# RMSNorm and matmul on one core: token tiles grouped by six where they were grouped by eight

## The chip, the core and the metric

The kernel runs on one core of one Trainium2 chip. The time is the device time of one execution in microseconds (us). The kernel before was run eight times; its median is 211.32 us, the lowest 211.1 and the highest 211.99.

## The reference

```
batch, seq, dim, out_dim = 16, 1024, 512, 768
rms = np.sqrt(np.mean(x ** 2, axis=-1, keepdims=True) + eps)
x_norm = x / rms * gamma
return np.matmul(x_norm, weight).astype(np.float32)
```

There are 16,384 tokens of 512 float32 values. Each token is divided by its root mean square, multiplied by gamma, and multiplied by a 512 x 768 weight matrix. The input is 33.5 MB, the weight 1.6 MB and the output 50.3 MB.

## The kernel before

A token tile is 128 tokens, one on each partition; there are NT = 128 of them. Tiles are worked off in pairs j = 0 to 63 (tile i belongs to pair i // 2).

For one pair the stages are these. GpSimd casts the two tiles from float32 to bf16 into a buffer `xb` (`cast`, line 86, four buffers of one pair). TensorE transposes the pair with two float32-wide transposes per tile, each word holding two bf16 values (`transpose_word`, line 113). VectorE copies the transposed pair from PSUM to `xT` (`evac`, line 120). ScalarE squares each tile of `x` with a running sum (`square`, line 90) and takes the root; VectorE takes the reciprocal (lines 94 and 96). TensorE multiplies each tile with the bf16 weights, which carry gamma, in four steps of 128 rows, 512 and 256 columns wide (`matmul`, line 147). ScalarE finishes the even tiles and VectorE the odd ones: the product times the reciprocal root goes to the output tile `ot` in SBUF (`scale`, lines 130 and 132).

Loads and stores move a group of tiles at once. In `rows` (line 54) a group of n tiles is laid out so that each partition holds n consecutive tokens: a load is 128 rows of n x 2 KB and a store 128 rows of n x 3 KB, each row contiguous in HBM. The group size G is 8, so a full load has rows of 16 KB and a full store rows of 24 KB. The first two and the last two groups of eight are cut into smaller transfers by the table `parts` (line 45). The pool `xin` has five buffers of eight tiles for loads, `out` three buffers of eight tiles for stores (lines 58 and 65).

All loads and all stores, and the two loads of the weights, are issued by the SP engine, one after the other in program order, on one DMA queue. SP waits before a store until the last tile of its group is finished (`store`, line 142), and everything that comes later in program order waits behind it. Loads are placed by `load_until(2 * j + AHEAD)` at the top of the loop over pairs (line 259), with AHEAD = 20: the load that begins at tile s comes in program order at the top of pair (s - 18) / 2. Before the loop, tiles 0 to 23 are requested (lines 185 to 189).

The order of the instructions is the written one (`tc.manual_schedule()`, line 177). In the loop, pair j casts pair j + 3, takes the norms of pair j + 1, and feeds the transposes of pair j + 2 in between its own matmuls (lines 258 to 277). The last pair's two tiles are finished in two column parts each (lines 280 to 286).

Of the kernel before, what the change touches and what calls it, by code (L numbers as in the profile page):

```python
# [12 lines left out]
F32 = mybir.dt.float32  # L13
# [5 lines left out]
def kernel(  # L19
# [9 lines left out]
    P = 128  # L29

    x = x.flatten_outer_dims()
    out = out.flatten_outer_dims()
    N, D = x.shape
    _, O = out.shape
    K = D // P
    NT = N // P
    NP = NT // 2
    G = 8
    NG = NT // G
    AHEAD = 20  # L40
    WIDE = 512

    parts = {0: [1, 2, 1, 2, 2], 1: [4, 4], NG - 2: [4, 4], NG - 1: [2, 2, 2, 1, 1]}
    first, size = {}, {}
    for g in range(NG):
        i = g * G
        for n in parts.get(g, [G]):
            for t in range(n):  # L50
                first[i + t], size[i + t] = i, n
            i += n

    def rows(ap, i):
        return ap[first[i] * P:(first[i] + size[i]) * P, :].rearrange("(p t) d -> p t d", t=size[i])

    singles = ctx.enter_context(tc.tile_pool(name="singles", bufs=1))
    xin = ctx.enter_context(tc.tile_pool(name="xin", bufs=5))
    xbp = ctx.enter_context(tc.tile_pool(name="xb", bufs=4))
    junk = ctx.enter_context(tc.tile_pool(name="junk", bufs=2))  # L60
    stats = ctx.enter_context(tc.tile_pool(name="stats", bufs=4))
    xt_pool = ctx.enter_context(tc.tile_pool(name="xt", bufs=4))
    tpsum = ctx.enter_context(tc.tile_pool(name="tpsum", bufs=2, space=bass.MemoryType.PSUM))
    opsum = ctx.enter_context(tc.tile_pool(name="opsum", bufs=3, space=bass.MemoryType.PSUM))
    outp = ctx.enter_context(tc.tile_pool(name="out", bufs=3))

    x_tiles, xb_tiles, tp_tiles, rstd_of, xT_tiles, o_tiles = {}, {}, {}, {}, {}, {}

    def held(tiles, i, n=1):
        return tiles[i // G][:, i % G:i % G + n, :]  # L70

    def load(i):
        if i // G not in x_tiles:
            x_tiles[i // G] = xin.tile([P, G, D], F32, name="xt")
        nc.sync.dma_start(out=held(x_tiles, i, size[i]), in_=rows(x, i))  # L75

    starts = [i for i in range(NT) if first[i] == i]
# [1 line left out]
    def load_until(i):  # L79
        while starts and starts[0] < i:  # L80
            load(starts.pop(0))

    def cast(i, engine, n=1):
        if i // 2 not in xb_tiles:
            xb_tiles[i // 2] = xbp.tile([P, 2, D], BF16, name="xb")
        engine.tensor_copy(out=xb_tiles[i // 2][:, i % 2:i % 2 + n, :], in_=held(x_tiles, i, n))  # L86

    def square(i, ssq):
        jk = junk.tile([P, D], BF16, name="jk")
        nc.scalar.activation(out=jk, in_=held(x_tiles, i)[:, 0, :], func=AF.Square, accum_out=ssq)  # L90
# [44 lines left out]
        return opsum.tile([P, 2, WIDE], F32, name="ops").rearrange("p a b -> p (a b)")  # L135

    def out_tile(i):
        if i // G not in o_tiles:
            o_tiles[i // G] = outp.tile([P, G, O], F32, name="ot")
        return o_tiles[i // G][:, i % G, :]  # L140

    def store(i):
        if i == first[i] + size[i] - 1:
# [14 lines left out]
    def finish_tile(i, acc, engine):  # L158
        scale(engine, out_tile(i), acc[:, :O], rstd_of[i])
        store(i)  # L160
# [16 lines left out]
    with tc.manual_schedule():  # L177
# [102 lines left out]
        for i in (NT - 2, NT - 1):  # L280
            for lo, hi, engine in ((0, WIDE, nc.scalar), (WIDE, O, nc.vector)):
                a = accumulator()
                for k in range(K):
                    matmul(i, k, a, lo, hi)
                scale(engine, out_tile(i)[:, lo:hi], a[:, lo:hi], rstd_of[i])
            store(i)
# [35 lines left out]
```

## Time and profile before

| what | value |
|---|---|
| median of eight runs | 211.32 us |
| the profiled execution's own time | 211.18 us |
| its span, first to last instruction | 209.4 us |
| lies around the span | 1.8 us |
| mean granted TensorE clock | 0.991 |
| bytes moved by the DMA engines | 85.69 MB |

The profile follows one execution. The span is what the instruction records cover; the time is 1.8 us longer. PE is TensorE's matmul and transpose work, DVE is VectorE, ACT ScalarE, POOL GpSimd, and SP the engine that only issues transfers here; SPq is its sequencer. A group of instructions is one row: line, engine, operation, what it writes and reads, count, busy time and mean length, and then the idle time before it with what ended it. The rows of DMA issues give the count, the size of each and the median time from issue to landing. "DMA share" in a table by stretches is the mean busy share of the core's 16 DMA engines; it can come out a little over 1 because packets on one engine overlap slightly.

### The profile page before, as it was taken

The numbers are of one execution on the slowest core, as the hardware profiler recorded it, in microseconds if no ns is written. First come the engines' busy times: TensorE is split into PE (matmuls) and PEld (weight loads), VectorE is DVE, ScalarE is ACT, GpSimd is POOL, SyncE is SP. The second block draws the span as 40 slices with busy tenths as digits, with TensorE's granted clock in tenths as the row PEclk, the third lists the DMA queues.
The fourth block names the chain that finished last, engine by engine and source line by source line (L and its number), as shares of the span: only waits on it lengthen the run. The fifth ranks groups of instructions, "written<-read, shape, count | busy, mean of one in ns | idle before, by whom it ended". The sixth has DMA issues, their size and how long they took to land.

```text
span 209.4 us, 3573 instructions
## 1 busy us (share of the span) xinstructions
PE 199.5 (95%) x1272; PEld 137.5 (66%) x1297; DVE 111.6 (53%) x204; ACT 158.2 (76%) x388; POOL 66.5 (32%) x71
## 2 busy tenths in 40 slices
PE   7999999999999999999999999999999999999970
PEld 2466767666776667766777666766677666776640
DVE  2555654564465456545644654565466456545630
ACT  4589787788778777877887787778778777877840
POOL 1157432516232433323242332324233315050000
PEclk9999999999999999999999999999999999999996
DMA  6999999999999999999999999999999999998984
GB/s 215 409 426 424 382 441 412 425 423 450 419 412 443 421 433 415 427 444 410 440 416 433 427 435 430 430 424 426 435 423 432 415 436 390 420 447 350 410 355 163
DMA packets 8070, 85.69 MB, mean 409 GB/s; under 512 B 1138, under 2 KB 1140, under 8 KB 3956
## 3 DMA queue, kind: packets, MB, share of 16 engines
q1 hardware_dynamic: 7776, 85.46, 97.3%
q8 instruction: 10, 0.16, 0.3%
q10 hardware_dynamic: 276, 0.00, 0.1%
q14 instruction: 8, 0.07, 0.1%
HBM read 35.13 MB, written 50.33 MB: 408 GB/s over the span
## 4 chain that ended last, share of the span: by engine, by line
PE 92%; DMA 3%; issue 1%; DVE 0%; SPq 0%; DVEq 0%
PE ops L147 79%; PE tp L113 13%; DMA w_f<-in_weight_dram 3%; SPq L75 0%; DVE w_bf L132 0%; DVE ot L132 0%; DVEq L132 0%
## 5 line engine op out<-in xcount | busy, mean ns | idle before, releaser
L147 PE MATMUL ops<-w_bf,xT 128*128 128x512 bf16 (+1 forms) x999 | 192.5, 324 | 1.4 <-DVE w_bf L132 0.2
L147 PEld LDWEIGHTS <-xT 128*128 128x128 bf16 x1024 | 100.2, 98 | 56.5 <-DVE xT L120 0.8
L86 POOL CAST xb<-xt 128x1024 bf16<-128x1024 f32 (+1 forms) x65 | 65.8, 1020 | 120.3 <-DMA xt<-in_x_dram 64.8
L120 DVE COPY xT<-tp 128x1024 bf16<-128x1024 bf16 (+1 forms) x67 | 44.6, 667 | 80.9 <-PE tp L113 80.9
L130 ACT ACTIVATE ot<-ops,rstd 128x768 f32<-128x768 f32 (+1 forms) x65 | 58.1, 895 | 37.6 <-PE ops L147 36.8
L90 ACT ACTIVATE jk<-xt 128x512 bf16<-128x512 f32 x128 | 78.7, 619 | 1.3 <-DMA xt<-in_x_dram 1.3
L113 PE MATMUL tp<-ident_f,xb 128*128 128x128 f32 x256 | 69.0, 273 | 0.6 <-DVE xb L86 0.5
L132 DVE TENSOR_SCALAR ot<-ops,rstd 128x768 f32<-128x768 f32 (+1 forms) x65 | 64.5, 992 | 2.9 <-PE ops L147 2.8
L113 PEld LDWEIGHTS tp<-ident_f,xb 128*128 128x128 f32 x256 | 35.7, 141 | 5.3 <-issue 1.1
L90 ACT ACTIVATION_READ_ACCUMULATOR jk<-xt 128x1 f32 x128 | 24.4, 191 | 0.0
L94 ACT ACTIVATE rms<-ssq,eps_sb 128x2 f32<-128x2 f32 (+1 forms) x64 | 18.9, 296 | 2.0
L96 DVE RECIPROCAL rstd<-rms 128x2 f32<-128x2 f32 (+1 forms) x64 | 10.0, 156 | 3.2 <-ACT rms L94 3.1
L202 PE MATMUL ops<-warm 128*128 128x512 bf16 x15 | 5.0, 479 | 1.2 <-DVE eps_sb L195 1.2
L130 ACT ACTIVATE w_bf<-w_f,g_sb 128x768 bf16<-128x768 f32 x2 | 1.9, 936 | 2.2 <-DMA w_f<-in_weight_dram 2.2
L202 PEld LDWEIGHTS <-warm 128*128 128x128 bf16 x15 | 1.5, 113 | 2.9 <-DVE eps_sb L195 1.2
L184 ACT ACT_TABLE_LOAD x1 | 1.3, 1283 | 1.8 <-issue 1.8
L86 DVE CAST xb<-xt 128x512 bf16<-128x512 f32 x2 | 0.9, 428 | 2.4 <-DMA xt<-in_x_dram 2.4
L132 DVE TENSOR_SCALAR w_bf<-w_f,g_sb 128x512 bf16<-128x512 f32 (+2 forms) x3 | 1.4, 485 | 1.4 <-DMA w_f<-in_weight_dram 1.4
L193 DVE MEMSET warm<- 128x256 uint32 x1 | 0.3, 272 | 0.9 <-PEq L303 0.9
L224 PEld LDWEIGHTS tp<-ident_f,g_row 2*128 2x128 f32 x2 | 0.3, 201 | 0.3 <-DVE xT L120 0.3
L224 PE MATMUL tp<-ident_f,g_row 2*128 2x2 f32 x2 | 0.4, 265 | 0.1
masks.py:199 POOL TENSOR_SCALAR_AFFINE_SELECT ident_f<-ident_f 128x128 f32<-128x128 f32 x1 | 0.3, 293 | 0.1
(7 smaller groups left out, 0.8 us busy)
## 6 DMA issues: line engine op xcount, KB each, us to landing
out_dram<-ot SPq DMA_DIRECT2D x12, 3072.0 KB, 15.9
xt<-in_x_dram SPq DMA_DIRECT2D x12, 2048.0 KB, 20.3
out_dram<-ot SPq DMA_DIRECT2D x4, 1536.0 KB, 11.3
out_dram<-ot SPq DMA_DIRECT2D x6, 768.0 KB, 8.9
xt<-in_x_dram SPq DMA_DIRECT2D x4, 1024.0 KB, 14.1
xt<-in_x_dram SPq DMA_DIRECT2D x6, 512.0 KB, 14.7
w_f<-in_weight_dram SPq DMA_DIRECT2D x2, 768.0 KB, 6.9
out_dram<-ot SPq DMA_DIRECT2D x4, 384.0 KB, 8.8
```

What stands on the lines that cost most here:

```text
L86: engine.tensor_copy(out=xb_tiles[i // 2][:, i % 2:i % 2 + n, :], in_=held(x_tiles, i, n))
L90: nc.scalar.activation(out=jk, in_=held(x_tiles, i)[:, 0, :], func=AF.Square, accum_out=ssq)
L94: nc.scalar.activation(out=rms[:, :n], in_=ssq[:, :n], func=AF.Sqrt, scale=1.0 / D, bias=eps_sb)
L96: nc.vector.reciprocal(out=rstd[:, :n], in_=rms[:, :n])
L113: nc.tensor.transpose(out=tp_tiles[j][:, t, h, :], in_=words[:, lo:lo + P], identity=ident_f)
L120: nc.vector.tensor_copy(out=dst[:, t:t + n, :], in_=src[:, t:t + n, :])
L130: nc.scalar.mul(out=dst, in_=src, mul=r)
L132: nc.vector.tensor_single_scalar(out=dst, in_=src, scalar=r, op=mybir.AluOpType.mult)
L147: nc.tensor.matmul(out=acc[:, lo:hi], lhsT=xT_tiles[i // 2][:, i % 2, k // 2, :, k % 2], rhs=w_bf[:, k, lo:hi], start=(k == 0), stop=(k == ...
L184: nc.scalar.preload_act_table(AF.Sqrt)
L202: nc.tensor.matmul(out=spare[:, :WIDE], lhsT=warm[:, :P], rhs=warm, start=True, stop=True)
L224: nc.tensor.transpose(out=gp[:, c, :], in_=g_row[:, :, c], identity=ident_f[:2, :2])
```

## The change

The group size becomes 6, and the grouping is no longer by i // 8 but by an explicit list. A full load now has rows of 12 KB and a full store rows of 18 KB. `xin` goes from five buffers of eight tiles to six of six (80 KB to 72 KB per partition), `out` from three of eight to four of six (72 KB per partition both times). AHEAD stays 20.

The list of transfers was 1, 2, 1, 2, 2, 4, 4, then twelve of 8 (tiles 16 to 111), then 4, 4, 2, 2, 2, 1, 1. It becomes 1, 2, 1, 2, 2, 4, then eighteen of 6 (tiles 12 to 119), then 2, 2, 2, 1, 1. That is 29 loads and 29 stores instead of 26 and 26. The new dictionary `base` gives the first tile of the buffer that a tile lives in; a buffer holds one inner list of `parts`.

```diff
-    G = 8
-    NG = NT // G
+    G = 6
     AHEAD = 20
     WIDE = 512
...
-    parts = {0: [1, 2, 1, 2, 2], 1: [4, 4], NG - 2: [4, 4], NG - 1: [2, 2, 2, 1, 1]}
-    first, size = {}, {}
-    for g in range(NG):
-        i = g * G
-        for n in parts.get(g, [G]):
+    parts = [[1, 2, 1, 2], [2, 4]]
+    while sum(map(sum, parts)) + G < NT - 2:
+        parts.append([G])
+    parts += [[2, 2, 2], [1, 1]]
+    first, size, base = {}, {}, {}
+    i = 0
+    for group in parts:
+        start = i
+        for n in group:
             for t in range(n):
-                first[i + t], size[i + t] = i, n
+                first[i + t], size[i + t], base[i + t] = i, n, start
             i += n
+    assert i == NT
...
-    xin = ctx.enter_context(tc.tile_pool(name="xin", bufs=5))
+    xin = ctx.enter_context(tc.tile_pool(name="xin", bufs=6))
...
-    outp = ctx.enter_context(tc.tile_pool(name="out", bufs=3))
+    outp = ctx.enter_context(tc.tile_pool(name="out", bufs=4))
...
     def held(tiles, i, n=1):
-        return tiles[i // G][:, i % G:i % G + n, :]
+        t = i - base[i]
+        return tiles[base[i]][:, t:t + n, :]
 
     def load(i):
-        if i // G not in x_tiles:
-            x_tiles[i // G] = xin.tile([P, G, D], F32, name="xt")
+        if base[i] not in x_tiles:
+            x_tiles[base[i]] = xin.tile([P, G, D], F32, name="xt")
         nc.sync.dma_start(out=held(x_tiles, i, size[i]), in_=rows(x, i))
...
     def out_tile(i):
-        if i // G not in o_tiles:
-            o_tiles[i // G] = outp.tile([P, G, O], F32, name="ot")
-        return o_tiles[i // G][:, i % G, :]
+        if base[i] not in o_tiles:
+            o_tiles[base[i]] = outp.tile([P, G, O], F32, name="ot")
+        return o_tiles[base[i]][:, i - base[i], :]
```

## The prediction

> **What bounds the kernel now.** I read the page first: the span, the busy shares, the DMA row, the chain.
>
> ```profile
> span 209.4 us, 3573 instructions
> PE 199.5 (95%) x1272; PEld 137.5 (66%) x1297; DVE 111.6 (53%) x204; ACT 158.2 (76%) x388; POOL 66.5 (32%) x71
> DMA  6999999999999999999999999999999999998984
> DMA packets 8070, 85.69 MB, mean 409 GB/s; under 512 B 1138, under 2 KB 1140, under 8 KB 3956
> q1 hardware_dynamic: 7776, 85.46, 97.3%
> PE 92%; DMA 3%; issue 1%; DVE 0%; SPq 0%; DVEq 0%
> ```
>
> Two resources are full at once. TensorE makes up 92% of the chain, and the 16 DMA engines are 90% busy or more in nearly every slice. The table by stretches says how close they are and what happens at the end:
>
> ```profile
> core 0: us, PE busy (x) PEld busy (x) DVE busy (x) ACT busy (x) POOL busy (x), PEclk, DMA share, GB/s
> 84.30:96.45 12.15, 12.10 (x81) 8.52 (x81) 6.75 (x12) 9.67 (x25) 4.17 (x4) 1.00 1.01 427
> ...
> 192.50:194.00 1.50, 1.50 (x13) 1.04 (x11) 0.32 (x2) 0.91 (x2) 0.00 (x0) 1.00 0.59 238
> ...
> 199.00:200.00 1.00, 1.00 (x8) 0.61 (x7) 0.00 (x0) 0.84 (x1) 0.00 (x0) 1.00 0.73 301
> ...
> 206.10:208.40 2.30, 0.00 (x0) 0.00 (x0) 0.00 (x0) 0.00 (x0) 0.00 (x0) 0.50 0.10 40
> ```
>
> Eight tiles take TensorE 12.15 us (1.519 each); their 3 MB store and 2 MB load take the DMA engines the same 12.15 us. In 192.5 to 200 some engines run dry before a store arrives. But in 206.1 to 208.4 the share is 0.10, or 1.6 engines of 16: one or two engines are still writing when the others are done. The last row says when they finish: the last store, issued by SP at 203.39, lands 5.2 us later, at 208.6, and the span ends there.
>
> ```profile
> 203.39 0.33 SPq L144 DMA_DIRECT2D out_dram<-ot  x1
> out_dram<-ot SPq DMA_DIRECT2D x1, 384.0 KB, 5.2
> ```
>
> The landing records, one per engine and transfer, show the same: 14 of the 16 parts of the last store land by 206.5, two at 208.2 and 208.6. These two fell behind at 23 to 37 us and have no idle time afterwards: the last five stores land on them at 201.0, 203.0, 204.8, 206.7, 207.7, then 208.6, spaced by packet time alone. So the end is set by the sum of the packets on the two late engines, not by TensorE, whose last product is at 202.8.
>
> **What one row costs.** The page counts 7776 packets on the queue. That is 54 transfers (26 loads, 26 stores, 2 of weights) times 128 rows and 16 completion writes: a row is one packet whatever its length, and an engine gets 8 rows of each transfer. The trace's single packets have these median lengths: stores of 3, 6, 12 and 24 KB 121, 234, 460 and 912 ns; loads of 2, 4, 8 and 16 KB 84, 159, 313 and 611 ns; a completion 9 ns. Two 12 KB stores take 920 against 912, so a store row costs 8 ns beside its bytes; for loads two of 8 KB against one of 16 gives 15, two of 4 KB against one of 8 gives 5.
>
> **The change, part by part.**
>
> *Six more transfers.* Three loads x 8 rows x 5 to 15 ns = 0.12 to 0.36 us; three stores x 8 x 8 = 0.19; six completions x 9 = 0.05. Sum on every engine, the late ones included: 0.36 to 0.60; I take 0.5 us, as most of the new load rows are long, where the overhead was 15. Here the Trainium skill speaks against the change: "DMA: Bandwidth & Descriptors", on the anatomy of one DMA (measured for transfers issued by GpSimd), gives about 2.0 us fixed per transfer plus bytes over 436 GB/s. By it a middle group before would take 2 x 2.0 + 5.24 MB / 436 = 16.0 us, where the trace has 12.15, and six more transfers would cost 12 us. The fixed part is not paid on the engines here, since the next transfer is already queued. The rows decide: 0.5.
>
> *Middle groups.* Store 8 x 686 ns (18 KB, on the line through 12 and 24) + load 8 x 461 (12 KB as for stores) + 18 ns = 9.20 us; the same arithmetic gives 12.20 before, where 12.15 was seen, so 9.16. TensorE needs 6 x 1.519 = 9.11. The DMA engines fall behind by about 0.05 us per group, 0.8 over 18 groups; 0.3 of that is won back in the pieces that are gone.
>
> *Loads are requested later.* Before, the load of tile s is released by the store that ends at tile s - 25, so 24 tiles ahead (36.5 us); after, by the one that ends at s - 19, 18 ahead (27.3 us). That is 9.1 us less lead. In return eight fewer tiles of loads are queued in front when the request is made: 8 x 611 ns = 4.9 us. What lead is spare now?
>
> ```profile
> 47.48 0.38 SPq L75 DMA_DIRECT2D xt<-in_x_dram  x1
> xt<-in_x_dram SPq DMA_DIRECT2D x1, 2048.0 KB, 20.1
> 67.70 1.04 POOL L86 CAST xb<-xt 128x1024 bf16<-128x1024 f32 x1 [2.96 <-DMA xt<-in_x_dram]
> ```
>
> Tile 48 is requested at 47.48, lands at 67.6, and is cast until 68.7. Its transposes come with tile 44, which starts at about 76.3 (tile 16 at 33.75, then 1.519 each): 7.5 us spare, 7.2 in later groups. After: 7.2 - 9.1 + 4.9 = 3.0, falling to about 2.2 by the last group. TensorE should not wait. GpSimd waits longer for the load and has 2 us idle per pair to do so.
>
> *Buffers.* A load into `xin` reuses a buffer read at least 12 tiles before (six of six, 18 ahead); an output buffer is written again 18 tiles, 27 us, after its store is issued, which lands in about 12 to 16. Cost nothing; if a store took over 27 us, ScalarE's and VectorE's writes and then TensorE would wait.
>
> *Start.* Still tiles 0 to 23 are requested in eight loads. Tiles 12 and 13 come in a load of six rather than four and land 16 x 77 ns = 1.2 us later, so their cast moves from 18.0 to 19.2; their transposes come with tile 9, at 23. Nothing. The load of tile 24 is two tiles shorter, 1.2 us earlier.
>
> *Tail.* Tiles 114 and 115 now leave with 119. For the 14 engines that are idle at 193, work from there is 5.5 + 3 x 1.89 + 2 x 0.98 = 13.1 us, to 206.7 instead of 206.1. The late two have 3.9 us of work left at 192.8 (the store of 112 to 115 lands at 197.2); they will have 3.9 - 1.9 + 0.5 = 2.5, so they don't run dry and merely end 0.5 later.
>
> Sum: the profiled 211.18 + 0.5 = 211.7; the median stands 0.14 higher, so **211.8 us**, +0.2%. Within 0.2% (0.42 us) is about what measurement can't tell from no change.
>
> **Rivals.**
>
> *Long packets go away (faster).* The 16 KB loads average 625 ns against a median of 611; several groups took over 1 us at 19 to 21 us and again at 29 to 33, just when the two engines fell behind. The 8 KB loads average 313.6 against 313. The skill's same page, among latency facts, reports rates falling where rows are a large power of two apart in HBM, measured from 512 KB; 16 KB is a power of two and 12 is not, but no trace here shows that this matters. If 12 KB loads have no long packets, 14 ns x 96 rows = 1.3 us are saved: 211.32 + 0.5 - 1.3 = 210.5. The bound is the punctual engines: at most 2.1 - 0.6 = 1.5 us off, 209.8. Against it: long packets also hit the 24 KB stores (mean 920), and some sit beside instruction fetches, which stay.
>
> *The rows are slower than the line says, and loads come late (slower).* If a group takes over 9.11 + 3.0 / 18 = 9.28 us (1.4% over my 9.16), the spare lead is used up within the run and TensorE waits for GpSimd's cast. At 2% over, 18 x 0.18 = 3.3 us more packet time on engines that never idle: 211.32 + 0.5 + 3.3 = 215.1; at 1.4%, 214.1. Against it: 12 KB rows were seen, at 460.
>
> *It does nothing measurable.* Where an engine falls behind depends on which one meets a fetch or a long packet; half a microsecond less of that hides the extra rows: 211.3.
>
> **How the numbers follow.** My forecast 0.50 (it straddles the bound: slower 0.27, same 0.23); long packets gone 0.25 (faster 0.19, same 0.06); late loads 0.15, slower; nothing 0.10 (same 0.06, slower 0.04). Faster 0.19, same 0.35, slower 0.46. The forecast's own range is 211.3 to 212.3. For 8 in 10 the range goes from 210.3 (most of the faster case) to 213.6 (just short of the late case).
>
> **What would show it.** Right: TensorE without waits on `xb`; middle loads landing about 15.5 to 16.5 us after their issue; 18 KB packets near 686 ns and 12 KB ones near 461; one or two engines writing alone for some 2 us at the end. Wrong: TensorE waiting for line 86 in the middle (late loads); all 16 engines ending together near 206.7 (long packets gone); DMA share falling in the middle.

## The result, and the profile after

The changed kernel takes 212.51 us (median of 11 runs, 212.31 to 213.21) where the kernel before takes 211.26 us (32 runs). The ratio is 1.0058, with a 95% interval of 1.0044 to 1.0072: about 1.2 us slower. The forecast was 211.8 us, 0.5 us slower. The result lies inside the range given for 8 in 10 (210.3 to 213.6), and 0.2 us above the forecast's own range (211.3 to 212.3).

These lines of the changed kernel's page answer to those shown of the kernel before:

```profile
span 210.6 us, 3587 instructions
PE 199.7 (95%) x1272; PEld 137.9 (65%) x1297; DVE 111.7 (53%) x204; ACT 158.3 (75%) x388; POOL 64.7 (31%) x71
DMA  6999999999999999999999999999999999996993
q1 hardware_dynamic: 8640, 85.46, 97.0%
PE 92%; DMA 1%; DVE 1%; ACT 1%; issue 1%
```

The span grew by 1.2 us, and no engine's own work grew by more than 0.2 us. The queue's 8640 packets are 60 transfers x (128 + 16), as counted. Their time per DMA engine is 97.0% of 210.6 = 204.3 us, against 97.3% of 209.4 = 203.7.

TensorE did not wait for GpSimd's casts: its list of waits has no `xb` in it.

```profile
PE ops L207 <- DVE eps_sb L200: 1.2, 1, 1.2
PE tp L229 <- DVE xT L125: 0.3, 1, 0.3
```

SP issues the last store at the same moment as before, 203.39, and it lands 6.2 us later instead of 5.2. So TensorE is not late; what was lost shows between the last product and the last byte.

```profile
203.39 0.33 SPq L149 DMA_DIRECT2D out_dram<-ot  x1
out_dram<-ot SPq DMA_DIRECT2D x1, 384.0 KB, 6.2
```

The table by stretches of the changed kernel, with the columns as before:

```profile
192.50:194.00 1.50, 1.50 (x13) 1.04 (x11) 0.32 (x2) 0.92 (x3) 0.00 (x0) 1.00 0.64 238
...
206.10:208.40 2.30, 0.00 (x0) 0.00 (x0) 0.00 (x0) 0.00 (x0) 0.00 (x0) 0.73 0.45 178
208.40:210.60 2.20, 0.00 (x0) 0.00 (x0) 0.00 (x0) 0.00 (x0) 0.00 (x0) 0.50 0.02 8
```

The engines again run dry near 193, all 16 now write until about 207, and a few go on alone. The landing records give both parts. The median engine's part of the last store lands at 207.28 (206.45 before), the last one's at 209.64 (208.56 before).

### The profile page after: what moved, and what is told of

Read it like the earlier page. It is cut to its first block, busy times and chain, and to the rows that moved or that the text cites. A ratio compares the mean times of both kernels' runs of the same rounds, so it can differ in the third digit from the quotient of the medians.

```text
span 210.6 us, 3587 instructions
## 1 busy us (share of the span) xinstructions
PE 199.7 (95%) x1272; PEld 137.9 (65%) x1297; DVE 111.7 (53%) x204; ACT 158.3 (75%) x388; POOL 64.7 (31%) x71
## 3 DMA queue, kind: packets, MB, share of 16 engines
q1 hardware_dynamic: 8640, 85.46, 97.0%
## 4 chain that ended last, share of the span: by engine, by line
PE 92%; DMA 1%; DVE 1%; ACT 1%; issue 1%
PE ops L152 77%; PE tp L118 13%; DMA xt<-in_x_dram 1%; PE ops L207 1%; DVE ot L137 1%; ACT ot L135 0%; DVE xT L125 0%; ACT jk L95 0%; DVE xb L91 0%; PE tp L229 0%; ACT rms L99 0%; DVE rstd L101 0%
## 5 line engine op out<-in xcount | busy, mean ns | idle before, releaser
L91 POOL CAST xb<-xt 128x1024 bf16<-128x1024 f32 (+1 forms) x65 | 64.0, 1017 | 126.6 <-DMA xt<-in_x_dram 110.0
L99 ACT ACTIVATE rms<-ssq,eps_sb 128x2 f32<-128x2 f32 (+1 forms) x64 | 18.9, 295 | 2.0
L207 PE MATMUL ops<-warm 128*128 128x512 bf16 x15 | 5.6, 526 | 1.2 <-DVE eps_sb L200 1.2
```

Of the source, the lines that this page charges most:

```text
L99: nc.scalar.activation(out=rms[:, :n], in_=ssq[:, :n], func=AF.Sqrt, scale=1.0 / D, bias=eps_sb)
L207: nc.tensor.matmul(out=spare[:, :WIDE], lhsT=warm[:, :P], rhs=warm, start=True, stop=True)
```

## The experiments

Each kernel was timed beside the kernel before on the same chip. Ratios are to that kernel, with 95% intervals. Four explanations were open: the added transfers cost packet time on late engines that never idle (ROWS); or the cost comes from the cut of the first transfers (HEAD), from that of the last group (TAIL), or from the shorter lead of the loads (LEAD). That late engines set the end at all had to be shown first.

**One store left out in the middle, in each kernel**

```diff
-        if i == first[i] + size[i] - 1:
+        if i == first[i] + size[i] - 1 and first[i] != 60:
```

(56 in place of 60 in the kernel before.)

> The changed kernel without the store of tiles 60 to 65 (left out: those 768 output rows are never written), so every DMA engine has 5.5 us less to do in the middle of the run. LATE ENGINES (two or three engines that never idle set the end): the lateness is used up, all 16 parts of the last store land within 0.5 us of each other near 207.3 in the profile, and the time falls by 2.3 us to 210.2. TENSOR ENGINE BOUND (the end is the last product plus a fixed tail): no change, 212.5.

> The kernel before without the store of tiles 56 to 63 (left out: those 1024 output rows are never written), 7.3 us less on each DMA engine in the middle. LATE ENGINES: falls by about 2.1 us to 209.2, ending where the punctual engines end (206.5 in the profile). TENSOR ENGINE BOUND: no change, 211.3. If both hold their ends by late engines, the changed kernel without its store ends 0.6 to 0.9 us after this one, which is what the six-tile store at tile 119 costs the punctual engines.

Measured: 0.9952 (0.9929 to 0.9975), 210.54 us, and 0.9912 (0.9891 to 0.9932), 209.44 us. TensorE does the same work in both, so in the two full kernels it does not set the end. The last store of the kernel before, without the one in the middle, and the stretch after it:

```profile
203.38 0.33 SPq L144 DMA_DIRECT2D out_dram<-ot  x1
out_dram<-ot SPq DMA_DIRECT2D x1, 384.0 KB, 3.1
...
206.10:208.40 2.30, 0.00 (x0) 0.00 (x0) 0.00 (x0) 0.00 (x0) 0.00 (x0) 0.50 0.00 0
```

It is issued at the same time as ever and lands after 3.1 us instead of 5.2, on all 16 engines between 206.37 and 206.51; nobody writes alone at the end. In the changed kernel all parts land between 207.55 and 207.73, in a profile whose last store was issued 0.37 later (203.76), so at 207.4 on the same clock. Both come where the expectations had put the punctual engines, 206.5 and near 207.3. Late engines hold both kernels up, by some 2 us.

**The last group of six cut in two and four**

```diff
+    parts[-1] = [2, 4]
     parts += [[2, 2, 2], [1, 1]]
```

> The changed kernel with the last six-tile group (tiles 114 to 119) cut into a load and store of 2 and of 4 tiles, so that 114 and 115 leave earlier, as before the change. 30 loads, 30 stores. ROWS: 0.1 to 0.2 us more than the changed kernel, 212.6 to 212.7. TAIL: 0.6 us less than the changed kernel, 211.9. HEAD: 212.5 to 212.7.

Measured: 1.0051 (1.0034 to 1.0069), 212.53 us, as the changed kernel. Its last store lands on the median engine at 206.38, as before the change, so the six-tile store at tile 119 does delay the punctual engines by 0.9 us; but it lands on the last at 209.91.

```profile
203.34 0.33 SPq L150 DMA_DIRECT2D out_dram<-ot  x1
out_dram<-ot SPq DMA_DIRECT2D x1, 384.0 KB, 6.6
...
206.10:208.40 2.30, 0.00 (x0) 0.00 (x0) 0.00 (x0) 0.00 (x0) 0.00 (x0) 0.70 0.18 72
```

Three engines write alone at the end: their parts land at 208.30, 208.63 and 209.91. TAIL is out: the 0.9 us that the cut takes off the punctual engines was not on the path that ends last.

**The head of the kernel before, groups of six after tile 24**

```diff
-    parts = [[1, 2, 1, 2], [2, 4]]
-    while sum(map(sum, parts)) + G < NT - 2:
-        parts.append([G])
-    parts += [[2, 2, 2], [1, 1]]
+    parts = [[1, 2, 1, 2, 2], [4, 4], [8]] + [[G]] * 16 + [[2, 2, 2], [1, 1]]
```

(with five load and three store buffers of eight tiles)

> The changed kernel with the head of the kernel before: tiles 0 to 23 move in transfers of 1, 2, 1, 2, 2, 4, 4, 8, then sixteen of 6 and the same tail; buffers five and three of eight tiles. Still 29 loads and 29 stores. ROWS (every transfer adds its row overhead on engines that never idle, and which engine is late is chance): as the changed kernel, 1.006 of the kernel before, 212.5 us. HEAD (the changed kernel loses 0.5 to 0.9 us on all engines at 27 to 31 us because of how the first transfers are cut): 211.7 to 212.0, ratio 1.002 to 1.0035. TAIL (the last six-tile store delays the end): 212.5.

Measured: 1.0081 (1.0059 to 1.0103), 213.23 us: worse than the changed kernel, so this head does not bring the time back. But the loss that HEAD speaks of is there. In the changed kernel the DMA rate drops at 24 to 32 us while the engines stay busy; the second line is the same stretch of the kernel before:

```profile
24.00:32.00 8.00, 7.95 (x54) 5.64 (x54) 5.06 (x9) 6.07 (x17) 3.07 (x3) 1.00 1.02 358
...
24.00:32.00 8.00, 7.95 (x54) 5.64 (x54) 5.06 (x9) 6.06 (x17) 3.90 (x4) 1.00 1.03 429
```

That is 358 GB/s at a share of 1.02 against 429 at 1.03. (The kernel before has a shorter drop at 20 to 24 us, 372 GB/s at 0.99.) With the other head the drop is at 52 to 60 instead, and larger:

```profile
24.00:32.00 8.00, 7.95 (x54) 5.64 (x54) 5.06 (x9) 6.01 (x17) 4.00 (x4) 1.00 1.02 406
52.00:60.00 8.00, 7.90 (x54) 5.58 (x54) 4.46 (x9) 6.14 (x16) 2.30 (x3) 1.00 0.99 329
```

In these stretches single 12 KB packets take up to 1.4 and 1.6 us. Since the drop moved and did not go away, the time of this run doesn't tell what the head is worth; the landings further down tell more. Added up over the run, packets exceed the medians of their sizes by 3.1 and 3.2 us per engine in the two profiles of the kernel before, 3.3 and 3.5 in those of the changed kernel, and 4.5 here. What sets off such a drop was not found.

**The same loads released 24 tiles ahead instead of 18**

```diff
-    AHEAD = 20
+    AHEAD = 22
```

> The changed kernel with AHEAD = 22 instead of 20: each middle load comes in program order one pair earlier, which puts it before a store instead of after it, so that it is released 24 tiles ahead, as before the change, instead of 18. Same 29 loads and 29 stores of the same sizes. ROWS: no change against the changed kernel, ratio 1.005 to 1.006; the middle loads' spare lead grows by 9.1 us less 3.7 us of longer queue. LEAD (the shorter lead, or the smaller stock of queued work, costs part of it): 0.3 to 0.7 us less, ratio 1.002 to 1.004.

Measured: 1.0044 (1.0031 to 1.0058), 212.47 us. The changed kernel had 1.0058, so LEAD would be worth some 0.3 us, and the intervals overlap: no gain is shown, and a few tenths are not excluded. The middle loads now land 18.9 us after their issue (first line; the changed kernel is the second), with more queued ahead of them.

```profile
xt<-in_x_dram SPq DMA_DIRECT2D x18, 1536.0 KB, 18.9
...
xt<-in_x_dram SPq DMA_DIRECT2D x18, 1536.0 KB, 15.5
```

**The transfers split, nothing else moved**

```diff
-        nc.sync.dma_start(out=held(x_tiles, i, size[i]), in_=rows(x, i))
+        n = size[i] // 2 if size[i] == G else size[i]
+        for t in range(0, size[i], n):
+            nc.sync.dma_start(out=held(x_tiles, i, size[i])[:, t:t + n, :], in_=rows(x, i)[:, t:t + n, :])
```

(and the stores likewise, in a kernel of their own.)

> The kernel before with each of its twelve eight-tile loads issued as two transfers of four tiles, back to back (rows of 8 KB at a pitch of 16 KB; same layout in SBUF, same place in the order, same stores). Nothing is released earlier or later. ROWS: 12 more transfers x (8 rows x 15 ns + 9 ns) = 1.5 us more on every engine, so on the late ones that set the end: 212.8, ratio 1.007. LEAD OR RELEASE (what costs in the changed kernel is when loads and stores are released, not their number): 1.000.

> The kernel before with each of its twelve eight-tile stores issued as two transfers of four tiles, back to back, when all eight tiles are finished (rows of 12 KB at a pitch of 24 KB). ROWS: 12 x (8 x 8 ns + 9 ns) = 0.9 us: 212.2, ratio 1.004. LEAD OR RELEASE: 1.000.

Measured: loads 1.0050 (1.0035 to 1.0065), 212.82 us; stores 1.0045 (1.0030 to 1.0060), 212.53 us. Twelve transfers more cost 1.06 us of loads or 0.95 us of stores, 0.088 and 0.079 each, with release and order unchanged: added transfers do cost time. The stores met their 0.9; the loads cost 1.06 where 1.5 was expected. In that profile two 8 KB packets (309 ns each at the median) stand against one of 16 KB (611), 7 ns more, so 15 ns was too much for a load row. The prices are not rows alone: per DMA engine the packets sum to 204.48 us (loads split) and 204.61 (stores split), 0.7 and 0.8 more than in the kernel before. In both profiles the latest engine is also further behind the mean at the last store (3.4 and 2.8 us; 1.9 and 2.3 in the two profiles of the kernel before). At these prices the change's three loads and three stores are worth 0.50 us. They cost 1.0 to 1.2.

**Both kernels once more**

> The changed kernel once more, for a second profile. If the slump of the DMA rate at 24 to 31 us belongs to this order of transfers, it is there again, with long 12 KB packets in it; if it was chance, it is gone or elsewhere. If the larger spread between the punctual and the late engines (5.4 us at the store of tiles 108 to 113, against 4.3 before) belongs to the kernel, it is again over 5 us and the last store again lands at about 209.6 us. Ratio 1.006 again.

> The kernel before once more, for a second profile. If the spread between engines and the place of the long packets belong to the kernel: spread of about 4.3 us at the store of tiles 112 to 115, last landing near 208.6, slow packets at 19 to 21 us again.

Measured: the changed kernel 1.0048 (1.0026 to 1.0069), 212.81 us, on a chip on which the kernel before takes 211.74. The drop is there again:

```profile
28.00:32.00 4.00, 3.95 (x27) 2.81 (x27) 2.53 (x5) 2.90 (x9) 0.30 (x1) 1.00 1.00 353
```

With two profiles each, the engines can be compared at a point of equal remaining work: the store of tiles 108 to 113 after the change, and that of 112 to 115 before it less 1.87 us, the packets of two tiles (8 x 234 ns).

| kernel | mean of 16 engines, us | latest engine, us | last store's last landing, us |
|---|---|---|---|
| before | 192.10 | 195.32 | 208.56 |
| before, again | 192.11 | 195.79 | 208.98 |
| changed | 192.71 | 196.45 | 209.64 |
| changed, again | 192.67 | 197.20 | 210.36 |

The mean engine is 0.58 us later, the latest 1.27, and the end 1.23. For the latest engine and the end, the two profiles of one kernel differ by 0.4 to 0.8 us among themselves, so 1.27 is not known to better than some tenths. Each DMA engine's packets sum to 203.73 and 203.80 us before, 204.23 and 204.45 after: 0.58 again. Of this 0.32 is the sum of the median lengths and 0.26 are longer packets.

The landings also show where the time is lost. From each landing I take off what the tiles queued up to it need at the medians of the kernel before, 0.611 us per tile loaded and 0.912 per tile stored. What is left is a lag, which can be compared at any time. Mean engine / latest engine, in us:

| at about | before | before, again | changed | changed, again |
|---|---|---|---|---|
| 50 us | 4.60 / 7.20 | 4.75 / 7.40 | 5.34 / 7.57 | 5.16 / 8.15 |
| 150 us | 5.39 / 7.80 | 5.42 / 7.94 | 6.32 / 8.48 | 6.26 / 8.93 |
| 193 us | 6.30 / 9.52 | 6.32 / 9.95 | 6.94 / 10.62 | 6.91 / 11.37 |

By 50 us, after the drop, the changed kernel is 0.57 us later on the mean engine and 0.56 on the latest. This belongs to the cut of its first transfers: from 20 to 50 us the mean lag grows by 1.7 to 2.2 us in the five profiles with this cut, whatever else was changed, and by 0.7 to 1.3 us in the nine others. So HEAD was right about that part of the cost, about half a microsecond on all engines, though a drop came elsewhere when the head was put back. From 50 to 150 us another 0.3 is added on both. After 150 us the mean engine's difference shrinks to 0.6, as the punctual engines of the kernel before run dry at 170 to 182 us, and the latest engine's grows by a further 0.4, to 1.26.

The records show one thing that can move a single engine so far. Between 60 and 180 us an engine's place among the others hardly moves from one transfer to the next (mostly by 0.1 us or less), but for steps. The largest steps come with the instruction fetches, which the page lists beside the kernel's own queue, ten of 16 KB in either kernel:

```profile
q8 instruction: 10, 0.16, 0.3%
```

Each of the six between 60 and 180 us sets one engine back by 1.2 to 1.8 us, in all four profiles. That of 175 to 176 us falls on one of the two latest engines each time. So which engine a fetch falls on can count as much as the whole change.

**Fewer transfers than before**

```diff
-    parts = {0: [1, 2, 1, 2, 2], 1: [4, 4], NG - 2: [4, 4], NG - 1: [2, 2, 2, 1, 1]}
+    loads = {0: [1, 2, 1, 2, 2], 1: [4, 4]}
+    stores = {NG - 2: [4, 4], NG - 1: [2, 2, 2, 1, 1]}
...
+    def rows(ap, i, n):
+        g = i // G * G
+        whole = ap[g * P:(g + G) * P, :].rearrange("(p t) d -> p t d", t=G)
+        return whole[:, i - g:i - g + n, :]
```

(In the first of the two, `stores` has all four entries of `parts`.)

> The kernel before, all groups of eight laid out in rows of eight tokens, and the last two groups loaded as two transfers of eight tiles instead of seven of 4, 4, 2, 2, 2, 1, 1; the first groups are loaded and all stores made in the same pieces as before (pieces of a longer row). 21 loads, 26 stores. ROWS, at the 0.088 us per load that the split loads measured: 5 x 0.088 = 0.44 us less: 210.9, ratio 0.998. CHANCE (the number of transfers has nothing to do with it): 1.000.

> As the one with merged loads, and the first two groups are also stored as two transfers of eight tiles instead of seven of 1, 2, 1, 2, 2, 4, 4. 21 loads, 21 stores. The queue then holds the load of tiles 24 to 31 in place of the first small stores, so the DMA engines should not run dry. ROWS: 0.44 + 5 x 0.079 = 0.84 us less: 210.5, ratio 0.996. If the engines run dry near 20 us: no gain or a loss. CHANCE: 1.000.

Measured: loads merged 1.0008 (0.9993 to 1.0022), 211.60 us: no gain. Loads and stores merged 0.9981 (0.9968 to 0.9995), 211.17 us: 0.4 us faster than the kernel before, and the fastest here, but half of the 0.84 that these prices gave. The profiles show two things that work against the gain. The small first loads are now pieces of long rows; the first tile is cast 0.2 to 0.5 us later, and SP's last store is issued at 204.5 and 203.9 instead of 203.4. And at 180 to 184 us engines run dry (share 0.75 in the first kernel, 0.90 in the second); by then their last loads have ended. In the second kernel the last store lands 3.8 us after its issue:

```profile
203.94 0.33 SPq L153 DMA_DIRECT2D out_dram<-ot  x1
out_dram<-ot SPq DMA_DIRECT2D x1, 384.0 KB, 3.8
```

The latest part lands at 207.8, 0.7 us behind the mean of the engines, where it was 1.9 and 2.3 in the kernel before.

**Groups of four**

```diff
-    G = 6
+    G = 4
...
-    parts = [[1, 2, 1, 2], [2, 4]]
+    parts = [[1, 2, 1], [2, 2]]
...
-    parts += [[2, 2, 2], [1, 1]]
+    parts += [[2], [1, 1]]
```

(with nine load and six store buffers of four tiles)

> The changed kernel with groups of four: 1, 2, 1, 2, 2, then twenty-nine of 4, then 2, 1, 1; nine load buffers and six store buffers of four tiles. 37 loads and 37 stores, 22 transfers more than the kernel before. Loads are released 20 tiles ahead. ROWS at the price of the split transfers and of the mean engine (0.085 us each): 22 x 0.085 = 1.9 us, 213.2, ratio 1.009. ROWS at the price that the change paid (1.1 us for 6, 0.19 us each, because the late engines lose more per transfer than the mean): 22 x 0.19 = 4.2 us, 215.5, ratio 1.020. GROUPS OF SIX ARE BAD IN THEMSELVES (their 12 KB loads meet long packets at 24 to 31 us): no slump there, and the price is the lower one.

Measured: 1.0054 (1.0040 to 1.0068), 212.76 us: 22 transfers more than before cost 1.1 us, no more than the six of the change. Both prices of ROWS are wrong for it. The packets sum to 204.7 us per engine, 0.9 more than before: 1.4 by median lengths, less 0.5 of longer packets, of which this kernel has 2.7 us. Its stretch where the changed kernel has its drop:

```profile
24.00:32.00 8.00, 7.95 (x54) 5.62 (x54) 5.06 (x9) 6.20 (x17) 2.11 (x3) 1.00 1.01 414
```

So the number of transfers alone doesn't give the time; the long packets and the distance of the latest engine count as much.

## Why the prediction was right in kind and short in size

*What bounds the kernel.* Right. Leaving one store out in the middle of either kernel moves the end by 1.9 to 2.1 us while TensorE's work stays, and with it the engines that wrote alone at the end are gone. One reading was incomplete: the late engines did not fall behind at 23 to 37 us only. In the profile that the prediction read, the latest was 2.3 us behind the mean at 171 us and 3.2 at 183; a fetch falls in between.

*What one row costs, and six more transfers: 0.5 us on every engine, the late ones included.* This is the term that was mis-sized. For the mean engine it held: 0.58 measured, 0.32 of it rows and completions (I had 0.36 to 0.60, too much for load rows) and 0.26 longer packets, which the step did not contain; that 0.5 came so near is in part luck. For the latest engine it was 1.27: 0.56 by 50 us, with the drop of the rate, 0.27 from 50 to 150 us, and 0.43 after that. The step had only the rows. A drop that holds up all engines stood in it at nothing, and the late engines' distance from the others was taken as given. What sets off the drop, and where the last 0.4 us come from, is not settled: the tail was tried and doesn't give it, the lead may hold a few tenths, and that the fetches fall differently on the late engines is a possible cause that no run tested.

*The fixed 2.0 us per transfer of the Trainium skill ("DMA: Bandwidth & Descriptors", anatomy of one DMA).* Rightly set aside: the estimate from it was 12 us for six transfers, and the split kernels measured 0.08 to 0.09 us per transfer.

*Middle groups: 686 and 461 ns, 9.16 us.* Measured 686 and 460 at the median; the latest landings of two loads in succession are 9.16 us apart (127.31 and 136.47).

*Loads are requested later, 3.0 us of spare lead, 2.2 at the end.* Right at first:

```profile
47.48 0.42 SPq L80 DMA_DIRECT2D xt<-in_x_dram  x1
xt<-in_x_dram SPq DMA_DIRECT2D x1, 1536.0 KB, 15.3
62.93 1.04 POOL L91 CAST xb<-xt 128x1024 bf16<-128x1024 f32 x1 [6.38 <-DMA xt<-in_x_dram]
```

This load of tiles 42 to 47 lands by 62.8; tile 42 is cast by 64.0 and transposed from tile 38's start on, at 67.2 by the prediction's pace: 3.2 us spare. The last full group, requested at 157.2, lands after 16.8 us; cast by 175.2 for a need at 176.5, it has 1.3 us left, and in the second profile 0.5, where 2.2 were forecast. TensorE never waited, but the margin was nearly used up.

*Buffers and start.* No wait on either reached TensorE.

*Tail.* Punctual engines 0.6 us later: measured 0.83. Late engines don't run dry: right, the latest lands its parts of the last stores at 204.1, 205.9, 207.8, 208.7 and 209.6, by packet time alone.

*The rivals.* Long packets did not go away; the 12 KB loads have more of them, 1.9 us per engine against 1.3 to 1.5 of the 16 KB loads. What the Trainium skill ("DMA: Bandwidth & Descriptors", latency and other measured facts) reports of HBM rows a large power of two apart, measured there from 512 KB, gets no support here at 16 against 12 KB. Late loads did not come about, with 0.5 to 1.3 us to spare. The rival that expected nothing measurable had named the fetches as what makes an engine late, which the landings bear out; its 211.3 us was too low.

## What to carry to other kernels

Where a kernel fills the DMA engines from end to end, read when each of the 16 parts of the last transfer lands, not the mean share: the end belongs to the latest engine. Here the last group cut in two brought the punctual engines 0.9 us and the kernel nothing. Count a transfer as its rows, here 0.05 to 0.09 us for 128 rows with the queue full, and not as a fixed latency. A regrouping that keeps the bytes can also make or move a stretch in which all packets are slow, and change how far the latest engine falls behind; here that cost more than the rows and could not be told from the sizes.

## What the runs showed of the hardware

One DMA engine is slower than the rest in its stores: between 60 and 190 us, 79 of the 24 KB store packets before the change are 3 to 10% longer than the median, by 44 ns on average, and nearly all follow one another; one engine has about 88 in that time. After the change it is 101 of 18 KB, of about 116, by 35 ns. The landings agree: in the changed kernel one engine falls some 0.3 us further behind with each store of six tiles, and not with the loads. That is 3.5 us in either kernel, enough to make an engine late, and equal before and after, so it does not explain the growth.

All 16 engines can slow down together while they stay busy: 358 GB/s at a share of 1.02 for 8 us, near the same place in both profiles of the changed kernel, and at 52 to 60 us with another head. In such a stretch the packets of one engine are 0.9 to 1.8 us longer in sum than by their medians.

Instruction fetches run on the same 16 engines: one of 16 KB, 0.9 to 1.1 us long in the records, sets the engine on which it falls back by 1.2 to 1.8 us while the queue is full.
